# Half sums of eight up weight pairs computed once, early, and stored; the down stage's row loads tied to its fifth step

## Chip, core and metric

The kernel runs on one core of a Trainium2 chip. The metric is device time in microseconds: the median of the runs, 2024.91 us here (3 runs, 2024.34 to 2026.39). The profiled execution is a run of its own, 2030.47 us, of which the profile's span covers 2028.8 us.

The core's engines, as the profile names them: PE (matrix products), PEld (its weight loads), DVE (vector), ACT (scalar, with the activation functions), POOL, and SP, which here only issues transfers. Transfers are issued from SP's, POOL's and ACT's queues. Each engine works its instructions off in a fixed order, and an instruction that waits holds up all that stand behind it on its engine.

## What is computed

One layer of a hybrid decoder on 1024 positions of width 1024, in float32. Cut to what matters:

```
h   = layer_norm(x)
u   = h @ w_in                       # -> conv branch, state-space branch, two gates
y_a = conformer_conv(...)            # 31-tap depthwise convolution, norm, product
y_b = state_space(...)               # 4 groups of 8 heads, in chunks of 128 positions
h   = layer_norm(alpha * h + (sigmoid(ga) * y_a + sigmoid(gb) * y_b) @ w_o)

u   = causal_dwconv3(h @ w_up)       # w_up: 1024 x 5632
gate, val = split(u)                 # 2816 columns each
h   = layer_norm(alpha * h + (silu(gate) * val) @ w_down)
```

## The kernel before

**Products.** A float32 operand is split into two float32r halves (a rounded copy made by ACT, and the remainder, made by a DVE subtraction); a product is the sum of three matrix products (`mm3`, lines 166 to 168). A full matmul works on 128x128 weights and 512 columns.

**Stages.** The positions are worked in two halves of 512. For each half run `ln_in`, `mixers` (all projections, the state-space groups, the convolution), `combine` (gates and the two branches put together, result `mixT`) and an output projection with the second norm. The calls in order are: `ln_in(0)`, `mixers(0)`, `combine(0)`, `ln_in(1)`, then `out_proj` of the first half (rows `r0_0` to `r0_3` in the pool `rows0`), `mixers(1)`, `combine(1)`, and the output projection of the second half inside `ffn_blocks`. Then comes the feed-forward part on all 1024 positions: `up_first`, 22 steps of `up_rest`, and `down`.

**The output stage of the first half.** `out_proj` works the 1024 output columns as two halves q = 0, 1. For each q it takes the four PSUM banks of the pool `pacc` (tag `acc`, four in all), adds up the products of four row blocks t in them with the weights `wo`, and then line 687 adds `r0_t`, the stored first-norm rows, to each bank and writes the sum over `r0_t`. Only this line frees a bank. q = 1 then takes the same banks, and the first products of `mixers(1)` (line 357) after it. The rows `r0_t` come from memory by line 670 on SP's queue.

**SBUF.** Pools opened and closed one after another on the same side lie on the same addresses. `combine` opens its pool at the end of the permanent buffers; its first tiles there are the three `gate` buffers and the two `yb` buffers, 2 KB per partition each. `rows0` opens at the same place: `r0_0`, `r0_1`, `r0_2`, `r0_3` of 4 KB per partition each, then the norm's two rows. The pools are made with `reuse_waits="tile"`: a tile waits for the earlier tiles whose bytes it takes over, and for no others.

**The up stage.** `w_up` and the block of rows are multiplied by a scheme with seven half-size products per step instead of eight. For step j it needs sums of the four quarters of two weight tiles `wup[2j]` and `wup[2j+1]` (512 columns each): `up_weights` loads both tiles (lines 839 and 844), makes four sums of 128x512 on DVE (lines 848 to 851) and splits the results (line 740 on ACT, line 741 on DVE). For the first eight steps (`LEAD`), two of the seven products, those with the unchanged first tile, are done ahead by `up_first`, which stores their sums; in those steps `up_rest` does five products, in the 14 others seven. At a step's end `up_rest` does the convolution and the gate on DVE and ACT and stores the results (lines 919 to 928), from POOL's queue mostly.

**The down stage.** Seven products p of eleven steps k each, in the same manner; `load(p, k)` loads a step's inputs from SP's queue (line 990 the stored up results, line 992 and on the weights). `load_rows(p)` is called at the step k = 4 of p = 0, 1, 2 and 4 and loads 4 quarters of the output's rows each time by line 953 on POOL's queue; with p = 2 also the last norm's two rows. Its transfers wait only for the buffers that they write.

**Order.** A planner lays down each engine's order ahead of the run from a model of the times and from priorities, which follow the program's order, shifted by `tc.high_priority`. A tile takes its buffer when the planner comes to it.

Of the kernel before, what the change touches and what calls it, by code (L numbers as in the profile page):

```python
# [8 lines left out]
F32 = mybir.dt.float32  # L9
# [7 lines left out]
P = 128  # L17
# [39 lines left out]
def kernel(  # L57
# [17 lines left out]
    def pool(name, bufs=1, **kw):  # L75
        return tc.tile_pool(name=name, bufs=bufs, reuse_waits="tile", **kw)
# [60 lines left out]
    h_scr = [dram.tile([HALF, D], F32, name=f"h_scr{i}") for i in range(2)]  # L137
    h1_scr = dram.tile([T, D], F32, name="h1_scr")
    first_scr = [dram.tile([2, P, HALF], F32, name=f"first_scr{j}") for j in range(LEAD)]
    NK = NF // 2  # L140
    b11_scr = [dram.tile([P, HALF], F32, name=f"b11_scr{k}") for k in range(NK)]
    b2_scr, t32_scr, t41_scr = (
# [601 lines left out]
    def ffn_blocks(tp, qp, mixT):  # L744
# [67 lines left out]
            "t4": lambda i: b2[0][:, i, 4:8, :],  # L812
        }

    def up_first(upp, fp, bl, j):

        if j < LEAD - 1:
            t = weights(wup[2 * j], f"ue{j}")
            w = [t[:, i, :] for i in range(2)]
        else:  # L820
            with tc.high_priority(offset=4000):
                st = wst.tile([P, D], F32, tag="st", name=f"st_ue{j}")
                SY.dma_start(st, wup[2 * j])
                w = [upp.tile([P, D], F32R, tag="o", bufs=3, name=f"ue{i}_{j}") for i in range(2)]
                A.copy(w[0], st)
                V.tensor_tensor(out=w[1], in0=st, in1=w[0].bitcast(F32), op=ALU.subtract)
        ps = bank(1)
        for q, block in enumerate(("b11", "b21")):
            product(ps, lambda i: w[i][:, q * HALF : (q + 1) * HALF], bl[block], q == 0)
            f = fp.tile([P, HALF], F32, tag="first", bufs=2, name=f"first{q}_{j}")  # L830
            A.copy(f, ps)
            A.dma_start(first_scr[j][1 - q], f)

    def up_weights(upp, j):


        with tc.high_priority(offset=2000):
            r1 = wst.tile([P, D], F32, tag="st", name=f"ra{j}")
            SY.dma_start(r1, wup[2 * j])
            if j:  # L840
                r2 = upp.tile([P, D], F32, tag="raw", bufs=3, name=f"rb{j}")
            else:
                r2 = wst.tile([P, D], F32, tag="st", name=f"rb{j}")
            SY.dma_start(r2, wup[2 * j + 1])
            a11, a12, a21, a22 = r1[:, :HALF], r1[:, HALF:], r2[:, :HALF], r2[:, HALF:]
            ue = None if j < LEAD else split_pair(wsp, r1, f"ue{j}")
            s3 = upp.tile([P, HALF], F32, tag="s3", name=f"s3_{j}")
            V.tensor_tensor(out=s3, in0=a11, in1=a21, op=ALU.add)
            V.tensor_tensor(out=a21, in0=a21, in1=a22, op=ALU.add)
            V.tensor_tensor(out=a11, in0=a21, in1=a11, op=ALU.add)  # L850
            V.tensor_tensor(out=a12, in0=a12, in1=a11, op=ALU.add)
            w24 = split_pair(wsp, r1, f"s24_{j}")
            w10 = split_pair(wsp, r2, f"s10_{j}")
            w3 = split_pair(upp, s3, f"s3_{j}", HALF, 2)
        return ue, w24, w10, w3
# [74 lines left out]
    def down(upp, dp):  # L930
# [16 lines left out]
        E, L = slice(0, HALF), slice(HALF, D)  # L947
        gb = []

        def load_rows(p):  # L950
            t0, cs = {0: (0, E), 1: (0, L), 2: (4, L), 4: (4, E)}[p]
            for t in range(t0, t0 + 4):
                G.dma_start(rs[t][:, cs], h1_scr[t * P : (t + 1) * P, cs])
            if p == 2:
# [136 lines left out]
        for p, (banks, first, then) in enumerate(products):  # L1091
            end = NK - LAST if p == 6 else NK
            for k in range(end):
# [1 line left out]
                for t in range(4):  # L1095
                    block(banks[t], w, t, first, k)
                if k == 4 and p in (0, 1, 2, 4):
                    load_rows(p)
            ws = {k: load(p, k) for k in range(end, NK)}
            for t in range(4):  # L1100
                for k in ws:
# [12 lines left out]
    hT = ln_in(0)  # L1114
    yT = mixers(0, hT)
    mixT = combine(0, hT, yT)
    hT = ln_in(1)
    with pool("rows0") as pl:
        rs = [pl.tile([P, D], F32, name=f"r0_{t}") for t in range(4)]
# [124 lines left out]
```

## Time and profile before

| | us |
|---|---|
| median of 3 runs | 2024.91 |
| profiled execution | 2030.47 |
| its span | 2028.8 |
| first half up to the output stage | 0 to 636 |
| output stage of the first half, with `ln_in(1)` | 636 to 686 |
| `mixers(1)`, `combine(1)`, second output stage | 686 to 1388 |
| the up steps | 1388 to 1806 |
| the down stage | 1806 to 2028 |

The stages are read from the first and last matmuls of their tiles in the timeline; they overlap a little. Neighbouring full matmuls start 0.227 us apart where PE runs on without a wait (16 of them from 654.83 to 658.23 us, so 15 steps in 3.40 us), though the profile shows each as 0.39 us long, since they overlap. Work on PE is therefore best counted in matmuls, and PE's idle time is what the profile shows between them.

### The profile page before, as it was taken

Reading aid. Unit: us, or ns where it says so; the run is one execution under the profiler, and the core shown is the slowest. Engines: PE = TensorE matmul, PEld = TensorE weight load, DVE = VectorE, ACT = ScalarE, POOL = GpSimd, SP = SyncE. Lnnn points to the kernel's source line nnn. Section 1 sums busy time; section 2 is a strip of 40 time slices with the busy share of each in tenths; the row PEclk is TensorE's granted clock in tenths of the full one; section 3 lists DMA queues with packets and bytes.
Section 4 is the critical chain, followed back from the end, with each engine's and each line's share of the span. In section 5 each row is a group of like instructions: output and inputs, shape, how many; then the busy total and the mean of one; then the engine's idle time right before and its main releaser. Section 6 shows DMA issues by size and latency. Waiting matters only on the chain.

```text
span 2028.8 us, 24542 instructions
## 1 busy us (share of the span) xinstructions
PE 1975.8 (97%) x9164; PEld 1622.4 (80%) x9164; DVE 1695.8 (84%) x2261; ACT 1017.4 (50%) x1480; POOL 175.5 (9%) x140
## 2 busy tenths in 40 slices
PE   7999999999999999999999999999999999999998
PEld 6888888888788888888888888887777777777886
DVE  7599999989766869999998976596897777788768
ACT  4465654556453356665454645364554534443432
POOL 2010101001400000110100130010000000030000
PEclk9999999999999999999999999999999999999999
DMA  6222233333546522222323354565342222367563
GB/s 219 94 64 93 79 103 104 99 104 101 175 131 220 194 94 73 91 81 77 126 89 104 109 167 139 186 234 202 135 172 83 99 107 102 101 252 252 176 225 109
DMA packets 96903, 272.20 MB, mean 134 GB/s; under 512 B 11088, under 2 KB 11088, under 8 KB 96784
## 3 DMA queue, kind: packets, MB, share of 16 engines
q1 hardware_dynamic: 88864, 246.78, 36.8%
q0 software_dynamic: 5616, 19.66, 2.5%
q10 hardware_dynamic: 2304, 4.20, 0.6%
q8 instruction: 72, 1.18, 0.2%
q14 instruction: 47, 0.39, 0.1%
HBM read 221.05 MB, written 49.55 MB: 133 GB/s over the span
## 4 chain that ended last, share of the span: by engine, by line
PE 72%; DVE 19%; DMA 4%; issue 3%; ACT 2%; SPq 0%; DVEq 0%; ACTq 0%
PE acc L166 19%; PE acc L167 19%; PE acc L168 19%; DVE c L420 6%; PE sm L168 3%; PE sm L166 3%; PE sm L167 3%; PE sm L534 2%; PE acc L357 1%; DVE xbc L375 1%; DVE fo L898 1%; DMA dr<-b_scr 1%; PE sm L515 1%; PE sm L192 1%; PE sm L523 1%
## 5 line engine op out<-in xcount | busy, mean ns | idle before, releaser
L420 DVE SCALAR_TENSOR_TENSOR c<-v,pc,c 128x512 f32<-128x512 f32 x480 | 374.9, 804 | 6.3 <-ACT c L409 4.9
L478 POOL TENSOR_TENSOR au<-seg_mv,head_of 128x1024 fp32r<-128x1024 f32 x32 | 76.4, 2388 | 959.1 <-PE sm L487 728.8
L166 PE MATMUL acc<-hT,w_c 128*128 128x512 f32 x352 | 141.0, 401 | 0.0
L167 PE MATMUL acc<-hT,w_c 128*128 128x512 f32 x352 | 140.6, 399 | 0.0
L168 PE MATMUL acc<-hT,w_c 128*128 128x512 f32 x352 | 138.4, 393 | 0.0
L898 DVE SCALAR_TENSOR_TENSOR fo<-u,pc,fo 128x1024 f32<-128x1024 f32 x88 | 111.4, 1279 | 7.5 <-ACT fo L894 7.4
L375 DVE SCALAR_TENSOR_TENSOR xbc<-u,pc,xbc 128x512 f32<-128x512 f32 x144 | 109.9, 775 | 0.7 <-ACT xbc L373 0.5
L166 PE MATMUL acc<-h1s,w_s 128*128 128x512 f32 x264 | 103.6, 396 | 6.3 <-ACT s L880 3.7
L167 PE MATMUL acc<-h1s,w_s 128*128 128x512 f32 x264 | 102.9, 390 | 0.0
L168 PE MATMUL acc<-h1s,w_s 128*128 128x512 f32 x264 | 102.8, 391 | 0.0
L167 PE MATMUL acc<-w_z,hT 128*128 128x512 f32 x256 | 100.8, 394 | 0.0
L166 PE MATMUL acc<-w_z,hT 128*128 128x512 f32 x256 | 100.8, 401 | 0.0
L168 PE MATMUL acc<-w_z,hT 128*128 128x512 f32 x256 | 100.7, 396 | 0.0
L1032 ACT CAST w_dn<-dr 128x1024 fp32r<-128x1024 f32 (+1 forms) x73 | 60.9, 842 | 75.8 <-DVE dr L962 37.8
L154 ACT CAST w_c<-st_c 128x1024 fp32r<-128x1024 f32 x50 | 52.5, 1051 | 88.9 <-PE acc L168 68.2
L1033 DVE TENSOR_TENSOR w_dn<-dr,w_dn 128x1024 fp32r<-128x1024 f32 (+1 forms) x73 | 69.8, 963 | 15.3 <-ACT w_dn L1032 15.1
L167 PEld LDWEIGHTS acc<-hT,w_c 128*128 128x128 f32 x352 | 66.1, 188 | 16.9 <-issue 3.9
L168 PEld LDWEIGHTS acc<-hT,w_c 128*128 128x128 f32 x352 | 66.1, 188 | 16.2 <-issue 2.6
L166 PEld LDWEIGHTS acc<-hT,w_c 128*128 128x128 f32 x352 | 66.1, 188 | 15.9 <-issue 2.6
L166 PE MATMUL acc<-h1b,w_ue 128*128 128x512 f32 x168 | 67.3, 400 | 11.1 <-ACT w_ue L740 8.4
L155 DVE TENSOR_TENSOR w_c<-st_c,w_c 128x1024 fp32r<-128x1024 f32 x47 | 60.5, 1288 | 20.2 <-ACT w_c L154 20.2
L740 ACT CAST w_s<-rb 128x1024 fp32r<-128x1024 f32 x22 | 23.0, 1048 | 98.4 <-PE sm L168 63.8
(353 smaller groups left out, 5755.4 us busy)
## 6 DMA issues: line engine op xcount, KB each, us to landing
st_c<-wcol SPq DMA_DIRECT2D x50, 512.0 KB, 3.5
st_z<-wz SPq DMA_DIRECT2D x32, 512.0 KB, 3.5
st_wo<-wo SPq DMA_DIRECT2D x24, 512.0 KB, 4.0
ra<-wup SPq DMA_DIRECT2D x22, 512.0 KB, 3.6
rb<-wup SPq DMA_DIRECT2D x22, 512.0 KB, 3.4
t_scr<-fo POOLq DMA_DIRECT2D x22, 512.0 KB, 3.8
dr<-t_scr SPq DMA_DIRECT2D x44, 256.0 KB, 3.5
dr<-wdown SPq DMA_DIRECT2D x38, 256.0 KB, 3.9
```

The costliest lines, as they stand in the source:

```text
L154: A.copy(w[:, 0, :], st)
L155: (eng or V).tensor_tensor(out=w[:, 1, :], in0=st, in1=w[:, 0, :].bitcast(F32), op=ALU.subtract)
L166: TE.matmul(ps, wa(0), xa(0), start=start, stop=False, skip_group_check=more)
L167: TE.matmul(ps, wa(0), xa(1), start=False, stop=False, skip_group_check=more)
L168: TE.matmul(ps, wa(1), xa(0), start=False, stop=stop, skip_group_check=more)
L375: V.scalar_tensor_tensor(out=o, in0=u[:, k : k + HALF], scalar=pc[:, wc + k : wc + k + 1], in1=o, op0=ALU.mult, op1=ALU.add,)
L420: V.scalar_tensor_tensor(out=accs[i], in0=v[:, k : k + HALF], scalar=pc[:, wc + k : wc + k + 1], in1=accs[i], op0=ALU.mult, op1=ALU.add,)
L478: G.tensor_tensor(out=au, in0=seg_mv[:, c, :].unsqueeze(1).to_broadcast([P, 8, P]), in1=head_of[:, g, :].unsqueeze(2).to_broadcast([P, 8, P]),
L534: TE.matmul(py[:, hs], m[:, h, :], xs[:, hs], start=True, stop=True)
L898: V.scalar_tensor_tensor(out=o, in0=u[:, k : k + T], scalar=pc[:, wc + k : wc + k + 1], in1=o, op0=ALU.mult, op1=ALU.add,)
L1032: A.copy(w[:, 0, cs], src)
L1033: V.tensor_tensor(out=w[:, 1, cs], in0=src, in1=w[:, 0, cs].bitcast(F32), op=ALU.subtract)
```

## The change

Before `ln_in(1)`, a new function `lead_sums` goes through the first eight pairs: it loads both weight tiles from POOL's queue into one buffer of 10 KB per partition (pool `sums`, one buffer), makes the four half sums on DVE, and stores all five halves in memory (1.25 MB per pair), again from POOL's queue. `up_weights` then loads the finished sums for these steps, in three transfers, instead of the two weight tiles and the four sums; for the other steps the code is the same, except that `r2` and `s3` are taken earlier, and that step 0 takes `r2` from the pool `up` like the others. In `down`, `load_rows` first copies four columns of the step's weight tile `w` into the rows it is about to load, on POOL; the loads then overwrite them, so that they wait for this copy, and the copy waits for `w`.

```diff
+    sums_scr = [dram.tile([P, 2 * D + HALF], F32, name=f"sums_scr{j}") for j in range(LEAD)]
...
+    def lead_sums(pl):
+
+        for j in range(LEAD):
+            r = pl.tile([P, 2 * D + HALF], F32, tag="sums", name=f"sums{j}")
+            for i in range(2):
+                G.dma_start(r[:, i * D : (i + 1) * D], wup[2 * j + i])
+            sums_of_pair(*(r[:, i * HALF : (i + 1) * HALF] for i in range(5)))
+            G.dma_start(sums_scr[j], r)
+
+    def sums_of_pair(a11, a12, a21, a22, s3):
+        V.tensor_tensor(out=s3, in0=a11, in1=a21, op=ALU.add)
+        V.tensor_tensor(out=a21, in0=a21, in1=a22, op=ALU.add)
+        V.tensor_tensor(out=a11, in0=a21, in1=a11, op=ALU.add)
+        V.tensor_tensor(out=a12, in0=a12, in1=a11, op=ALU.add)
+
...
         with tc.high_priority(offset=2000):
             r1 = wst.tile([P, D], F32, tag="st", name=f"ra{j}")
-            SY.dma_start(r1, wup[2 * j])
-            if j:
-                r2 = upp.tile([P, D], F32, tag="raw", bufs=3, name=f"rb{j}")
+            r2 = upp.tile([P, D], F32, tag="raw", bufs=3, name=f"rb{j}")
+            s3 = upp.tile([P, HALF], F32, tag="s3", name=f"s3_{j}")
+            if j < LEAD:
+                ue = None
+                SY.dma_start(r1, sums_scr[j][:, :D])
+                SY.dma_start(s3, sums_scr[j][:, 2 * D :])
+                SY.dma_start(r2, sums_scr[j][:, D : 2 * D])
             else:
-                r2 = wst.tile([P, D], F32, tag="st", name=f"rb{j}")
-            SY.dma_start(r2, wup[2 * j + 1])
-            a11, a12, a21, a22 = r1[:, :HALF], r1[:, HALF:], r2[:, :HALF], r2[:, HALF:]
-            ue = None if j < LEAD else split_pair(wsp, r1, f"ue{j}")
-            s3 = upp.tile([P, HALF], F32, tag="s3", name=f"s3_{j}")
-            V.tensor_tensor(out=s3, in0=a11, in1=a21, op=ALU.add)
-            V.tensor_tensor(out=a21, in0=a21, in1=a22, op=ALU.add)
-            V.tensor_tensor(out=a11, in0=a21, in1=a11, op=ALU.add)
-            V.tensor_tensor(out=a12, in0=a12, in1=a11, op=ALU.add)
+                SY.dma_start(r1, wup[2 * j])
+                SY.dma_start(r2, wup[2 * j + 1])
+                ue = split_pair(wsp, r1, f"ue{j}")
+                sums_of_pair(r1[:, :HALF], r1[:, HALF:], r2[:, :HALF], r2[:, HALF:], s3)
...
-        def load_rows(p):
+        def load_rows(p, w):
             t0, cs = {0: (0, E), 1: (0, L), 2: (4, L), 4: (4, E)}[p]
+            G.tensor_copy(
+                rows.rearrange("p (t n) -> p t n", n=D)[:, t0 : t0 + 4, cs.start : cs.start + 1],
+                w[:, 0, :4].bitcast(F32).unsqueeze(2),
+            )
             for t in range(t0, t0 + 4):
                 G.dma_start(rs[t][:, cs], h1_scr[t * P : (t + 1) * P, cs])
...
                 if k == 4 and p in (0, 1, 2, 4):
-                    load_rows(p)
+                    load_rows(p, w)
...
     mixT = combine(0, hT, yT)
+    with pool("sums") as pl:
+        lead_sums(pl)
     hT = ln_in(1)
```

## The prediction

> **What bounds the kernel now.** I read the page first: busy time, then the chain, then windows around the three places that the change touches.
>
> ```profile
> span 2028.8 us, 24542 instructions
> ...
> PE 1975.8 (97%) x9164; PEld 1622.4 (80%) x9164; DVE 1695.8 (84%) x2261; ACT 1017.4 (50%) x1480; POOL 175.5 (9%) x140
> ...
> PE 72%; DVE 19%; DMA 4%; issue 3%; ACT 2%; SPq 0%; DVEq 0%; ACTq 0%
> ```
>
> PE is busy for 97% of the span, and the change takes no matmul away. So all that can be gained is PE's idle time, 2028.8 - 1975.8 = 53 us, and what is done to other engines counts only where PE waits for it. The windows say where the idle time lies at the three places.
>
> ```profile
> core 0: us, PE busy (x) PEld busy (x) DVE busy (x) ACT busy (x) POOL busy (x), PEclk, DMA share, GB/s
> 636.50:661.80 25.30, 24.09 (x114) 19.78 (x112) 18.91 (x28) 8.62 (x13) 0.00 (x0) 1.00 0.87 332
> 661.80:686.30 24.50, 23.67 (x112) 19.79 (x113) 19.89 (x30) 6.81 (x10) 0.00 (x0) 1.00 0.49 176
> ...
> 1432.00:1512.00 80.00, 72.65 (x308) 56.52 (x307) 68.14 (x78) 40.18 (x50) 3.95 (x7) 1.00 0.44 155
> ...
> 1819.00:1832.00 13.00, 9.62 (x36) 7.55 (x35) 6.08 (x9) 5.70 (x10) 0.97 (x2) 0.83 0.94 346
> ```
>
> The first two rows are the output stage of the first half (q = 0, then q = 1): PE is idle for 1.2 and 0.8 us. The third is most of the eight short up steps: 7.4 us idle in 80, with DVE at 85%. The last is the start of the down stage: 3.4 us idle, the granted clock at 0.83, the DMA engines at 94%.
>
> **Part 1: the sums moved early, and what they stand in front of.** The buffer `sums` takes 10 KB per partition at the place where `combine` had three `gate` and two `yb` buffers of 2 KB: exactly those bytes. So the first load waits for the last reader of `gate`. After it, `rows0` opens at the same place: `r0_0` and `r0_1` lie wholly, `r0_2` in half on the bytes of `sums`. There is one buffer, so the eight pairs go one after another: load, four adds, store, and only when the store has landed the next load. The rows `r0_0` to `r0_2` can be loaded only after the eighth store. Who waits for them?
>
> ```profile
> 637.62 0.69 DVE L661 TENSOR_TENSOR mb<-mb,gl 128x512 f32<-128x512 f32 x1
> ...
> 661.82 1.86 DVE L687 SCALAR_TENSOR_TENSOR r<-r,acc 128x512 f32<-128x512 f32 x3
> ...
> 660.69 1.09 PE L192 MATMUL sm<-ident,x 128*128 128x128 f32 x8 [1.19 <-DVE x L230]
> 662.63 0.47 PE L166 MATMUL acc<-w_wo,mixT 128*128 128x512 f32 x1 [0.85 <-DVE r L687]
> ```
>
> The first row is the last use of `gate`: the chain of sums can start at 637.62 + 0.69 = 638.3 us. The last row is the point that decides: the first product of q = 1 waits for line 687, which frees the bank by adding `r0_t`. All four banks of `acc` are held by q = 0 until then, and the products of q = 1 and of `mixers(1)` take their banks from the same four. So from 662.6 us on PE stands until the eighth store has landed, a row has been loaded and line 687 has run, apart from 24 of the 32 transposes of `ln_in(1)`, which use other banks (8 took 1.09 us, so 3.3 us). `r0_3` lies beyond the buffer and may come early; one bank serves one row block of q = 1, and three weight buffers hold 18 of its products, 4.1 us; I count that as a bound only.
>
> Now the length of the chain. These are rows of transfers of the same kind:
>
> ```profile
> L928 POOL DMA_DIRECT2D t_scr<-fo x6: 531/531/533, 1552.0 to 1752.5; - x6
> ...
> DMA to landing us min/median/max: 2.9/3.5/4.3
> ...
> b_scr<-fo POOLq DMA_DIRECT2D x11, 256.0 KB, 2.3
> ...
> ra<-wup SPq DMA_DIRECT2D x22, 512.0 KB, 3.6
> ...
> r<-h_scr SPq DMA_DIRECT2D x4, 512.0 KB, 10.9
> ...
> L848 DVE TENSOR_TENSOR s<-ra,rb 128x512 f32<-128x512 f32 x22 | 15.1, 684 | 1.6 <-DMA rb<-wup 1.6
> ```
>
> - Loads: two of 512 KB, the second issued 0.53 us after the first. `ra`, the same tile from the same array, lands after 3.6 us: 0.5 + 3.6 = 4.1 us; with the slowest `t_scr` transfer (4.3) 4.8 us. I take 4.4.
> - Adds: 4 x 0.684 = 2.7 us, and a little for two hand-overs: 3.0 us. If DVE is busy with other work that stands ahead, up to 4.
> - Store of 1.25 MB: no such transfer is in the trace. Two `t_scr` stores of 512 KB, issued 0.53 us apart, are down after at most 0.5 + 4.3 = 4.8 us, and that for 1 MB: lower end 4.8 us. By the step from 256 KB (2.3) to 512 KB (3.5), 1.2 us for each 256 KB, it is 2.3 + 4 x 1.2 = 7.1 us: upper end. I take 5.4, near the pair, which is the nearest in size.
>
> One pair: 4.4 + 3.0 + 5.4 = 12.8 us; ends 4.1 + 2.7 + 4.8 = 11.6 and 4.8 + 4 + 7.1 = 15.9. The first pair meets the inputs of `ln_in(1)`, where 512 KB took 10.9 us to land (the row of `r`); I give it 18 us (14 to 20). The chain ends at 638.3 + 18 + 7 x 12.8 = 745.9 us. A row lands about 3.6 us later, line 687 takes 0.7: PE goes on at 750.2 instead of 662.6, 87.6 us late. Of that 3.3 us of transposes go off.
>
> The Trainium skill, "DMA: Bandwidth & Descriptors", section "Anatomy of one DMA — SWDGE (gpsimd) path", gives 2.0 us and the bytes by 436 GB/s for one transfer. By it, as an estimate, the load pair is 4.4 us and the store 5.0, so that the chain would end some 3 us earlier. Its rule for kernel authors, to overlap a transfer with work, speaks against a chain with one buffer.
>
> PE is also slow after a stop:
>
> ```profile
> 1391.46 0.79 PE L166 MATMUL acc<-h1b,w_ue 128*128 128x512 f32 x1 [2.73 <-ACT first L831]
> 1392.05 0.63 PE L167 MATMUL acc<-h1b,w_ue 128*128 128x512 f32 x1
> ...
> 1396.32 0.63 PE L168 MATMUL acc<-h1b,w_ue 128*128 128x512 f32 x1
> ```
>
> After 2.73 us of idle time, 12 steps took 1396.74 - 1391.46 = 5.3 us (the next matmul starts at 1396.74) where they take 12 x 0.227 = 2.7: 2.6 us lost. I add that once. **Part 1 costs 87.6 - 3.3 + 2.6 = +87 us**; with pairs at 11.6 and the first at 14 it is 87 - 4 - 8 = +75, less 4 if `r0_3` serves early: +71; with 15.9 and 20, +87 + 2 + 22 = +111.
>
> ```profile
> 740.12 3.34 POOL L478 TENSOR_TENSOR au<-seg_mv,head_of 128x1024 fp32r<-128x1024 f32 x1 [185.25 <-DVE seg_mv L328]
> ```
>
> What else is moved: the 32 adds (22 us of DVE) fall into a time in which DVE would wait for PE, so nothing. On POOL, `lead_sums` stands ahead of the `au` products of `mixers(1)`, the first at 740.12 us; they wait for `mixers(1)` itself and move with it, so nothing. SP's loads that the planner puts behind the `r0` loads wait with them; three weight buffers are filled ahead, which covers the first 3 x 24 matmuls of the next products, so nothing, or 4 us if it puts the `wo` loads behind. The stage after, `mixers(1)`, cannot make the time good: its work on PE is unchanged.
>
> **Part 2: the up steps.** The four adds per step go (4 x 0.684 = 2.7 us of DVE), for eight steps.
>
> ```profile
> 1466.97 0.54 POOL L919 DMA_DIRECT2D b_scr<-fo  x1 [12.38 <-DVE fo L909]
> ...
> 1527.79 0.55 POOL L919 DMA_DIRECT2D b_scr<-fo  x1 [11.26 <-DVE fo L909]
> ...
> PE acc L166 <- ACT s L880: 3.0, 4, 0.9
> PE acc L166 <- ACT u L883: 2.4, 2, 1.7
> PE sm L166 <- ACT w_s L740: 2.0, 3, 1.3
> ```
>
> Line 919 stores once per two steps: four steps take 60.8 us, 15.2 each, where 60 matmuls need 60 x 0.227 = 13.6. That is the 7.4 us of idle time, with the slow restarts. PE waits for ACT each time: 3.0 us for a bank's copy at line 880, which also stays in the long steps' order and may remain; the other 4.4 us are ACT held up behind DVE or behind the sums (line 740 casts `s3` right after line 848). I take -6 us for the eight steps: 4.4 us of these, and part of line 880. Bounds: 0, if the planner's new order keeps the waits, and 8 x 1.6 = -13. The loads grow from two to three per step and from 1 to 1.25 MB; the DMA share there is 0.44, so nothing.
>
> **Part 3: the row loads.**
>
> ```profile
> 1781.99 4.63 POOL L993 COPY c<-dr 128x512 f32<-128x512 f32 x4 [12.34 <-PE acc L168]
> ...
> 1805.38 3.78 POOL L953 DMA_DIRECT2D rows<-h_scr  x7 [1.70 <-PE sm L168]
> ...
> rows<-h_scr POOLq DMA_DIRECT2D x16, 256.0 KB, 8.2
> ...
> 1827.85 0.62 ACT L1032 CAST w_dn<-dr 128x512 fp32r<-128x512 f32 x1 [7.30 <-DMA dr<-b_scr]
> ...
> PE acc L166 <- ACT w_dn L1032: 3.4, 1, 3.4
> ```
>
> All 16 row loads (4 MB) are issued from 1805 us on, as the down stage begins; a stored up result comes 7.3 us late for its cast, and PE stands for 3.4 us and restarts slowly (2.6 us as above): 6.0 us. With the copies only four of the 16 can go at the start, 3 MB fewer ahead of the late load, about 9 us at the 346 GB/s of the last window row. So most of the 6.0 goes: I take -4, bounds 0 (the weights `c` and the remaining rows still crowd it) and -6. The four POOL copies of 128x4 cost less than the 128x512 copies of line 993 (four in 4.63 us, 1.2 each), off PE's path. Behind a waiting copy on POOL stand the row loads themselves, the last up pair's two stores and the last norm's rows; the stores are needed from p = 2 on, a product of 11 x 12 matmuls (30 us) after, so nothing; a row load that came late would hold up `then(t)` seven steps (19 us) later.
>
> **Sum.** 2030.5 + 87 - 6 - 4 = 2107.5 for the profiled execution, which lay 5.6 us above the median: **2102 us** for the median.
>
> **The rivals.**
>
> 1. *The wait is longer.* Pairs of 16 to 20 us, because stores of 10 KB rows are slow or DVE's laid-down order holds the adds behind waiting work. Against it: nothing else runs on the DMA engines once PE stands. With 18 us: +87 + 7 x 5.2 = +123, less 10: 2138 us.
> 2. *The wait is partly covered.* PE is given products of `mixers(1)` or of q = 1 during the chain. For it: the planner knows the wait. Against it: these need banks of `acc`, and only `r0_3` can free one. If half the wait went: 2025 + 43 - 10 = 2058 us.
> 3. *Faster: the rows do not wait for the sums*, because `rows0` does not come to lie on the buffer. Then the chain runs beside PE, and parts 2 and 3 are left: 2025 - 10 = 2015 us. It is decided by addresses alone: as soon as one of `r0_0` to `r0_2` shares bytes with `sums`, it falls. For it speaks only that the trace shows no addresses; the sizes (3 + 2 buffers of 2 KB, opened at the same place) speak against it.
> 4. *The change does less than it says*: the wait as forecast, but the new order gives no gain in parts 2 and 3: 2112 us, inside the forecast's range.
>
> **How the numbers follow.** Chances: the forecast (with 4) 0.74, longer wait 0.10, partly covered 0.07, faster 0.09. The forecast's own range: 2024.9 + 71 - 19 = 2077 to 2024.9 + 111 = 2136. With some us for a new order elsewhere, the range for 8 in 10 is 2071 to 2139: it leaves out rivals 2 and 3 nearly whole and half of rival 1. Runs of this kernel differ by 0.1%, so about 0.2% (4 us) can be told from no change. Faster by more: 0.09; within: 0.01; slower: 0.90.
>
> **What would show it.** Right: PE idle from about 666 to 750 us with line 687 and behind it the load of `r` as releaser; eight stores to `sums_scr` 12 to 13 us apart; the granted clock down in those slices; 14 instead of 22 of each add in the up stage, and its idle time (1432 to 1512 before) at 2 us or less; row loads in four groups, no wait of 3 us at the start of the down stage. Wrong: products of `mixers(1)` between 662 and 750 us, stores closer than 11 us, or the `r` loads ahead of the last of them.

## The result and the profile after

The changed kernel takes **2131.36 us** (median of 4 runs, 2130.93 to 2132.63), the kernel before 2025.65 us (4 runs); the ratio is **1.052** with a 95% interval of 1.0504 to 1.0535. The forecast was 2102 us, with a range of 2071 to 2139 us. Line numbers are those of the kernel that a row is from; in the changed kernel line 687 has become 688, line 166 has become 167 and line 919 has become 934.

The page of the changed kernel, busy time and chain of waits:

```profile
span 2130.9 us, 24619 instructions
...
PE 1979.5 (93%) x9164; PEld 1626.5 (76%) x9164; DVE 1701.1 (80%) x2261; ACT 1019.2 (48%) x1480; POOL 190.2 (9%) x168
...
PE 62%; DVE 24%; DMA 7%; issue 4%; ACT 2%; POOL 0%; SPq 0%; DVEq 0%; ACTq 0%; POOLq 0%
```

The span has grown by 102.1 us and PE's busy time by 3.7 only, so nearly all of it is PE standing still. The chain says through whom: PE has fallen from 72% to 62% of a longer chain, DMA has risen from 4% to 7%, DVE from 19% to 24%. The timeline of PE, then POOL, SP and DVE around the output stage of the first half (start, duration, idle time before and what ended it):

```profile
663.12 3.75 PE L193 MATMUL sm<-ident,x 128*128 128x128 f32 x16 [3.44 <-DVE x L231]
672.83 3.65 PE L193 MATMUL sm<-ident,x 128*128 128x128 f32 x16 [5.96 <-DVE x L231]
773.76 0.77 PE L167 MATMUL acc<-w_wo,mixT 128*128 128x512 f32 x1 [97.29 <-DVE r L688]
...
640.08 1.24 POOL L821 DMA_DIRECT2D sums<-wup  x2 [84.14 <-ACT mixT L183]
666.93 0.54 POOL L823 DMA_DIRECT2D sums_scr<-sums  x1 [25.62 <-DVE sums L829]
672.34 1.06 POOL L821 DMA_DIRECT2D sums<-wup  x2 [4.87 <-DMA sums_scr<-sums]
683.51 0.54 POOL L823 DMA_DIRECT2D sums_scr<-sums  x1 [10.11 <-DVE sums L829]
688.54 1.05 POOL L821 DMA_DIRECT2D sums<-wup  x2 [4.49 <-DMA sums_scr<-sums]
697.16 0.54 POOL L823 DMA_DIRECT2D sums_scr<-sums  x1 [7.57 <-DVE sums L829]
702.18 1.05 POOL L821 DMA_DIRECT2D sums<-wup  x2 [4.49 <-DMA sums_scr<-sums]
...
764.73 0.54 POOL L823 DMA_DIRECT2D sums_scr<-sums  x1 [7.36 <-DVE sums L829]
...
769.59 1.75 SPq L671 DMA_DIRECT2D r<-h_scr  x4
...
649.53 1.29 DVE L208 BATCH_NORM_STATS2 st_in<-x 128x6 f32<-128x512 f32 x2 [8.41 <-DMA x<-x]
...
656.90 0.68 DVE L826 TENSOR_TENSOR sums<-sums 128x512 f32<-128x512 f32 x1
...
680.34 0.69 DVE L826 TENSOR_TENSOR sums<-sums 128x512 f32<-128x512 f32 x1 [2.52 <-DMA sums<-wup]
...
694.00 0.69 DVE L826 TENSOR_TENSOR sums<-sums 128x512 f32<-128x512 f32 x1 [10.78 <-DMA sums<-wup]
...
772.93 0.69 DVE L688 SCALAR_TENSOR_TENSOR r<-r,acc 128x512 f32<-128x512 f32 x1 [8.49 <-DMA r<-h_scr]
```

Read from the bottom: line 688 waits for a row, the four rows are issued at 769.59 us, which is 4.9 us after the eighth store was issued at 764.73, and PE goes on 4.2 us later. Before the change the first product of q = 1 (the third row) went off at 662.63 us; now it goes off at 773.76, **111.1 us later**. The POOL rows are the chain itself: each load waits for the store before it. A whole pair of the steady part is 688.54 to 702.18: load to the first add 5.5 us, adds and hand-over 3.2, store 5.0. The DVE row's 10.78 us of idle time is a store and a load in one, not a load of 11 us. How long the chain's loads took to land, all 16 of line 821 (then all of the chain's stores, with their size and median):

```profile
DMA to landing us min/median/max: 3.9/4.7/8.6
...
sums_scr<-sums POOLq DMA_DIRECT2D x8, 1280.0 KB, 4.7
```

The windows of the changed kernel (stretch, its length, busy us per engine, granted clock, DMA share, GB/s): the stop, the short up steps from the first b_scr store to that of j = 6, and the start of the down stage.

```profile
661.80:780.00 118.20, 13.53 (x48) 11.09 (x49) 39.55 (x57) 5.18 (x10) 11.66 (x22) 0.54 0.55 204
1543.90:1636.40 92.50, 87.85 (x371) 69.89 (x370) 74.27 (x80) 48.89 (x60) 4.85 (x9) 0.98 0.46 154
1919.00:1945.00 26.00, 26.00 (x116) 21.51 (x116) 23.71 (x35) 13.17 (x24) 6.82 (x14) 1.00 0.90 304
```

```profile
1433.70:1527.80 94.10, 86.75 (x369) 68.18 (x368) 80.82 (x93) 48.84 (x62) 5.02 (x10) 1.00 0.42 149
```

The last row is the same up stretch of the kernel before: PE was idle there for 7.4 us, and now for 4.7. At the start of the down stage PE no longer stands at all. So both small gains came, and the stop outweighs them. Where the time lies, by the distance of the same event in the two traces:

| event | before | after | distance |
|---|---|---|---|
| first product of the output stage after line 688 | 662.63 | 773.76 | +111.1 |
| b_scr store of j = 0 | 1433.73 | 1543.87 | +110.1 |
| b_scr store of j = 6 | 1527.79 | 1636.43 | +108.6 |
| b_scr store of j = 20 | 1803.13 | 1911.70 | +108.6 |
| end (span) | 2028.8 | 2130.9 | +102.1 |

The last product of the second half's output stage, just ahead of the up stage, stands at +112.6. So Part 1 cost about 112 us, Part 2 gave back 4.0, and Part 3 gave back 6.5; the three add up to the span's 102.1 by the way they are read. The 4.0 is a rough figure: in the kernel with the early sums alone (below), whose up steps are those of the kernel before, the distance shrinks over the same stretch too, from 111.6 to 109.0 us.

### The profile page after: what moved, and what is told of

It reads as the page before. It is cut to its first block, busy times and chain, and to the rows that moved or that the text cites. A ratio compares the mean times of both kernels' runs of the same rounds, so it can differ in the third digit from the quotient of the medians.

```text
span 2130.9 us, 24619 instructions
## 1 busy us (share of the span) xinstructions
PE 1979.5 (93%) x9164; PEld 1626.5 (76%) x9164; DVE 1701.1 (80%) x2261; ACT 1019.2 (48%) x1480; POOL 190.2 (9%) x168
## 4 chain that ended last, share of the span: by engine, by line
PE 62%; DVE 24%; DMA 7%; issue 4%; ACT 2%; POOL 0%; SPq 0%; DVEq 0%; ACTq 0%; POOLq 0%
PE acc L167 16%; PE acc L168 16%; PE acc L169 16%; DVE c L421 8%; PE sm L167 3%; PE sm L168 3%; PE sm L169 3%; DMA sums_scr<-sums 2%; DMA sums<-wup 2%; DVE xbc L376 2%; PE acc L358 1%; PE sm L535 1%; DVE fo L913 1%; DMA st_wo<-wo 1%; PE sm L516 1%
## 5 line engine op out<-in xcount | busy, mean ns | idle before, releaser
L167 PE MATMUL acc<-w_wo,mixT 128*128 128x512 f32 x128 | 49.2, 402 | 98.5 <-DVE r L688 97.3
L167 PEld LDWEIGHTS acc<-w_wo,mixT 128*128 128x128 f32 x128 | 24.6, 193 | 104.8 <-issue 97.7
L155 ACT CAST w_wo<-st_wo 128x1024 fp32r<-128x1024 f32 x24 | 25.4, 1057 | 155.2 <-PE acc L169 145.9
L168 PEld LDWEIGHTS acc<-hT,w_c 128*128 128x128 f32 x352 | 66.1, 188 | 16.9 <-issue 3.8
L1052 DVE TENSOR_TENSOR w_dn<-dr,w_dn 128x1024 fp32r<-128x1024 f32 (+1 forms) x73 | 69.8, 963 | 11.2 <-ACT w_dn L1051 10.9
L169 PEld LDWEIGHTS acc<-hT,w_c 128*128 128x128 f32 x352 | 66.1, 188 | 16.1 <-issue 2.6
```

The lines of the kernel that those rows point to most:

```text
L155: A.copy(w[:, 0, :], st)
L167: TE.matmul(ps, wa(0), xa(0), start=start, stop=False, skip_group_check=more)
L168: TE.matmul(ps, wa(0), xa(1), start=False, stop=False, skip_group_check=more)
L169: TE.matmul(ps, wa(1), xa(0), start=False, stop=stop, skip_group_check=more)
L1052: V.tensor_tensor(out=w[:, 1, cs], in0=src, in1=w[:, 0, cs].bitcast(F32), op=ALU.subtract)
```

## The experiments

Eleven kernels ran, one of them twice. Times are medians, and ratios are against the kernel before on the same chip, with 95% intervals; a time without a ratio is one run.

| kernel | time | before there | ratio |
|---|---|---|---|
| early sums alone (not used) | 2139.18 | 2028.87 | |
| sums for four pairs | 2079.05 | 2028.87 | |
| buffer above the rows | 2086.63 | 2028.87 | 1.0284 (1.0269 to 1.0299) |
| row copies alone | 2023.60 | 2028.87 | 0.9971 (0.9960 to 0.9982) |
| row copies, one burst | 2023.54 | 2028.54 | 0.9978 (0.9968 to 0.9987) |
| three loads, no sums | 2024.27 | 2028.54 | 0.9984 (0.9976 to 0.9993) |
| above the rows, adds on POOL | 2058.18 | 2028.54 | 1.0141 (1.0127 to 1.0156) |
| above the rows, two buffers, late priority | 2066.03 | 2028.54 | |
| two buffers on the rows | 2099.68 | 2028.02 | |
| early, on POOL, in cc's bytes | 2035.88 | 2028.02 | 1.0036 (1.0022 to 1.0050) |
| the same, four pairs | 2027.06 | 2027.77 | 0.9993 (0.9984 to 1.0001) |
| row copies alone, again | 2022.82 | 2027.77 | 0.9977 (0.9967 to 0.9986) |

### Does the cost come from the sums, and from the bytes?

Two kernels ask whether Part 1 is alone to blame, and whether the shared bytes are the reason. The first is the kernel before with nothing but the early sums, whose results nobody reads:

```diff
     mixT = combine(0, hT, yT)
+    with pool("sums") as pl:
+        lead_sums(pl)
     hT = ln_in(1)
```

> The kernel before with only lead_sums put in; what it stores is not read. Theory: the wait alone, 112 us on the way from the output stage to the first products of mixers(1), and nothing given back: 2025.7 + 112 = 2138 us. Rival (the up steps or the row loads add to the loss, and the wait is smaller): below 2125 us.

It took 2139.18 us, 110.3 more than before, and PE goes on after line 688 at 773.83 us, where the changed kernel has 773.76:

```profile
773.83 0.77 PE L167 MATMUL acc<-w_wo,mixT 128*128 128x512 f32 x1 [97.49 <-DVE r L688]
```

So Part 1 makes the stop by itself. The second moves the buffer above the rows:

```diff
-    with pool("sums") as pl:
-        lead_sums(pl)
-    hT = ln_in(1)
     with pool("rows0") as pl:
+        with pool("sums") as sp:
+            lead_sums(sp)
+        hT = ln_in(1)
         rs = [pl.tile([P, D], F32, name=f"r0_{t}") for t in range(4)]
```

> The same work in the same program order, but the pool rows0 is opened before the pool sums, so that the buffer of the sums lies above the rows and r0_0 to r0_3 share no byte with it. Theory (shared bytes make the rows wait for the eighth store): the chain of eight pairs stays (12 to 16 us a pair from about 640 to 755 us), but PE goes on with q = 1 at about 663 us, and what is left is the gain of the other two parts: 2025.7 - 4 - 6.5 = 2015 us, ratio 0.995. Rival (the chain's transfers, its adds on DVE or its place in POOL's queue hold up the output stage, wherever the buffer lies): PE still stands for tens of us after 662 us, and the time stays above 2090 us.

The ratio is 1.0284: the 2015 us of the theory were missed by 72, and the rival's 2090 were not reached either. The wait for `r` is gone: the rows are issued at 646.40 us instead of 769.59, and the first product of q = 1 goes off at 664.57 us, 1.9 later than before the change. But another wait has come. SP's queue in the timeline of this kernel, PE's wait (total, times, longest), then ACT and DVE in the timeline:

```profile
646.40 6.55 SPq L671 DMA_DIRECT2D r<-h_scr  x4
...
PE acc L167 <- ACT w_z L155: 57.2, 1, 57.2
...
783.37 0.31 ACT L283 ACTIVATE sp<-sp 128x128 f32<-128x128 f32 x1 [64.55 <-DVE sp L282]
...
725.70 0.69 DVE L826 TENSOR_TENSOR sums<-sums 128x512 f32<-128x512 f32 x1 [10.09 <-DMA sums<-wup]
...
780.18 0.69 DVE L826 TENSOR_TENSOR sums<-sums 128x512 f32<-128x512 f32 x1 [10.83 <-DMA sums<-wup]
...
783.05 0.28 DVE L282 COPY sp<-sm 128x128 f32<-128x128 f32 x1
```

DVE is idle for ten us ahead of each of the last five pairs and does nothing else meanwhile, since the planner laid their adds in one row ahead of lines 281, 282 and 376, which `mixers(1)` needs. Line 282 takes its turn at 783.05 us, after the last add; ACT has waited for it for 64.6 us, and PE for ACT. The Trainium skill, "TensorE: Matmul & The Clock Gate", section "Architectural detail: the array is 16× 32×32, not 1× 128×128", says that ScalarE and VectorE take their instructions strictly in order. These rows agree. So the shared bytes carry the stop in the changed kernel, and the adds on DVE are a second cost behind it, here 57.2 us of PE's waiting, which the longer stop hid.

### Does the length of the chain set the stop?

Sums for four pairs instead of eight, the other four as before:

```diff
-        for j in range(LEAD):
+        for j in range(4):
             r = pl.tile([P, 2 * D + HALF], F32, tag="sums", name=f"sums{j}")
...
-            if j < LEAD:
+            if j < 4:
                 ue = None
```

> The changed kernel with four pairs in lead_sums instead of eight; steps 4 to 7 load their weight tiles and make the sums as before. Theory (the wait is the sum of the pairs, one after another): four pairs of 13.5 us less, 2131.4 - 54 = 2077 us, and about 2 us of the up steps' gain lost: 2079 us. Rival (a fixed hold-up, such as the planner's order of the output stage): about 2130 us.

PE goes on at 718.16 us, 55.6 us earlier than in the changed kernel; four pairs of 13.5 us are 54. The time is that of the theory.

```profile
718.16 0.77 PE L167 MATMUL acc<-w_wo,mixT 128*128 128x512 f32 x1 [43.73 <-DVE r L688]
```

Next, a second buffer at the same place:

```diff
-    with pool("sums") as pl:
+    with pool("sums", bufs=2) as pl:
         lead_sums(pl)
```

> The whole change with a second buffer beside the first, still on the bytes of the rows, adds on DVE. My theory: the stop on PE is as long as the chain, and the chain is load, adds, store one after the other only because there is one buffer; with two, the next load runs beside the store, 8 to 9 us a pair from the second pair on instead of 13.55, and PE goes on some 30 to 40 us earlier: 2090 to 2102 us. Rival: the transfers are bound by the DMA engines rather than by their order (2.25 MB a pair), or POOL's queue keeps them serial: above 2120 us.

It took 2099.68 us, and PE goes on 30.8 us earlier than with one buffer; both lie where the theory had them. PE and POOL in the timeline of this kernel, first and last store:

```profile
742.99 0.77 PE L167 MATMUL acc<-w_wo,mixT 128*128 128x512 f32 x1 [64.17 <-DVE r L688]
...
668.73 0.54 POOL L823 DMA_DIRECT2D sums_scr<-sums  x1 [26.70 <-DVE sums L829]
...
730.15 0.54 POOL L823 DMA_DIRECT2D sums_scr<-sums  x1 [9.97 <-DVE sums L829]
```

From the first to the eighth store it is 61.4 us, 8.8 for each pair where one buffer gives 13.4 to 16.6. The first store comes no earlier than with one buffer (666.93 us). So the time of a pair comes from load, adds and store standing one after another, and the first pair is another matter: its adds wait for their turn on DVE, which works at `ln_in(1)` then (see the part on what was mis-sized).

### Are Parts 2 and 3 worth what the distances say?

The row copies alone, in the kernel before:

```diff
-        def load_rows(p):
+        def load_rows(p, w):
             t0, cs = {0: (0, E), 1: (0, L), 2: (4, L), 4: (4, E)}[p]
+            G.tensor_copy(
+                rows.rearrange("p (t n) -> p t n", n=D)[:, t0 : t0 + 4, cs.start : cs.start + 1],
+                w[:, 0, :4].bitcast(F32).unsqueeze(2),
+            )
...
```

> The kernel before with only the copies in load_rows. Theory (fewer transfers at the start of the down stage): no wait of PE for a cast at the start of the down stage, 6 to 6.5 us less, 2019 us, ratio 0.997. Rival (the 6.5 us between the last up store and the end of the down stage came from the new order that follows from the up part): the wait of 3.4 us stays and the time is within 2 us of before.

The ratio is 0.9971, and 0.9977 when it ran again (below): 4.7 to 5.9 us less. PE has no wait left between 1800 and 1860 us, so the theory's sign is there. Why it gains is asked by the next kernel, which issues all 16 loads at the first of the four places:

```diff
-                if k == 4 and p in (0, 1, 2, 4):
-                    load_rows(p, w)
+                if k == 4 and p == 0:
+                    for q in (0, 1, 2, 4):
+                        load_rows(q, w)
```

> The row copies alone, but all 16 row loads are issued together, after the fifth step of the first product (each group still behind its copy). My theory: what the row loads alone gained (ratio 0.997) came from taking 3 MB away from in front of the late stored up result at the start of the down stage; then one burst, though it begins some 20 us later than before the change, meets other loads of the first and second product, and at least half of the gain goes: ratio 0.998 to 1.001, with waits on dr or w_dn somewhere between 1820 and 1860 us. Rival: the gain comes from the later start (the burst no longer falls on the last stored up results) or from the planner's new order, and spreading is worth nothing: ratio 0.997 again.

The ratio is 0.9978, and this interval and that of the copies alone overlap for the most part. The theory's waits between 1820 and 1860 us are not there: PE waits for nothing from 1800 to 1860 us. So the rival is right, and spreading is worth nothing that can be told here. POOL's timeline and a window of this kernel:

```profile
1809.32 10.27 POOL L952 COPY rows<-w_dn 128x4 f32<-128x4 f32 x4 [7.24 <-ACT w_dn L1036]
1819.53 4.34 POOL L957 DMA_DIRECT2D rows<-h_scr  x8
...
1820.00:1840.00 20.00, 20.00 (x90) 16.57 (x89) 16.00 (x26) 9.72 (x18) 9.87 (x19) 1.00 1.00 349
```

and the same window of the kernel before:

```profile
1820.00:1840.00 20.00, 16.62 (x61) 13.17 (x60) 12.07 (x19) 7.32 (x15) 2.70 (x5) 0.83 0.89 307
```

With one burst the DMA engines are full from 1820 to 1840 us, and PE does not stop once. The burst begins at 1819.53 instead of 1805.38 us, behind the six loads of stored up results that SP issues from 1808.69 us on, instead of ahead of them. Part of that is the copies' own length: four of them take 10.27 us here, where one takes 0.19 to 0.59 us in the kernel with the copies alone. That the later start is what counts fits these rows, but it is not shown by itself: the planner's new order, which the rival named beside it, came with the same edit. And in the kernel with the copies alone the first four loads start at 1810.74 us already, only 5.4 us later than before the change, with twelve fewer behind them.

For Part 2 there is the kernel before with three loads and no adds in the eight steps. It leaves out the sums, so it serves for the time alone:

```diff
...
+            if j < LEAD:
+                ue = None
+                SY.dma_start(r1, wup[2 * j])
+                SY.dma_start(s3, wup[2 * j][:, :HALF])
+                SY.dma_start(r2, wup[2 * j + 1])
...
```

> The kernel before with the up part alone: in the first eight up steps three loads (the half for s3 is read from the weights themselves) and no adds; the sums of the first eight pairs are left out, and neither the early sums nor the row copies are there. My theory, by the traces of the whole change (time between the last product of the second output stage and the up store of j = 20, 4.0 us shorter): about 4 us less, ratio 0.998, with 2.7 us less idle time on PE in the eight steps. The recorded prediction: 6 us less, 0.997. Rival: the planner's new order gives it back, 1.000.

The ratio is 0.9984: 3.2 us less (1.4 to 4.9). PE's waits from 1432 to 1528 us, where the kernel before had 7.4 us of them (3.0 for line 880, 2.4 for line 883, 2.0 for line 740), now lines 895, 898 and 741 of this kernel:

```profile
PE acc L167 <- ACT u L898: 3.7, 4, 1.5
PE sm L167 <- ACT w_s L741: 1.8, 2, 1.5
PE acc L167 <- ACT s L895: 0.7, 1, 0.7
```

The wait for the copy of `s` shrinks from 3.0 to 0.7 us. Those for `u` and `w_s` stay: of the 3.7 us for `u`, 1.5 lie at 1433.87 us, ahead of the first `b_scr` store (1434.97 us), so that the stretch itself, from that store to the one of j = 6, holds 2.2 where it held 2.4 before. Together that is 4.7 us, as in the changed kernel. So the adds had held up the copy of `s`; what holds the other two was not tried.

### Can the sums be had for nothing?

If the stop is a matter of place and engine, a version should exist in which only the gains are left. The first try keeps the buffers above the rows, takes two, gives the sums a lower priority for the planner, and gives the adds to POOL:

```diff
+        with pool("sums", bufs=2) as sp:
+            with tc.high_priority(offset=-1500):
+                lead_sums(sp)
...
-            sums_of_pair(*(r[:, i * HALF : (i + 1) * HALF] for i in range(5)))
+            sums_of_pair(*(r[:, i * HALF : (i + 1) * HALF] for i in range(5)), G)
```

> The whole change with the sums taken off both waits: two buffers, above the rows so that no byte is shared with r0, and the 32 adds on POOL instead of DVE. My theory: what was left at 1.028 with the buffer above the rows was DVE held by adds ahead of the products of the next mixers; with the adds on POOL (1.61 us each by the POOL adds of the same size in the combine stage, 6.5 us a pair; about 11 us a pair with the transfers, so the chain ends near 740 us, when POOL's first au product is due) nothing is held: the up steps' 4 and the row loads' 6 us are left, ratio 0.995 (2015 us). Rival: POOL's chain runs past 740 us and holds the au products, or POOL's adds slow DVE: 1.00 to 1.02.

The ratio is 1.0141, and the theory missed. The rival's range holds it, but the longest wait has a cause that neither named. ACT's timeline in this kernel:

```profile
727.20 0.19 ACT L373 COPY u<-u_halo 128x3 f32<-128x3 f32 x1
753.03 0.69 ACT L374 ACTIVATE xbc<-acc,pc 128x512 f32<-128x512 f32 x1 [25.65 <-DMA sums_scr<-sums]
```

It is the first mechanism once more, with another tile. In the built program the two buffers reach to byte 168,288 of a partition, and one of the first `xbc` tiles of `mixers(1)` begins at byte 168,000. ACT waits for the last store, 25.7 us. (One buffer at this place ends at 158,048, which is why the kernel above did not meet it.) It is not the whole loss: the first product of `mixers(1)`, ahead of this wait, already stands at 699.53 instead of 686.33 us. The same two buffers with the adds left on DVE:

```diff
+        with pool("sums", bufs=2) as sp:
+            with tc.high_priority(offset=-1500):
+                lead_sums(sp)
```

> As the version with the buffer above the rows, but with two buffers and with the sums at a lower priority for the planner, adds still on DVE. My theory (DVE held by the adds in its laid-down order until their loads come): the chain is shorter (store beside load, 8 to 9 us a pair) and the adds of pairs 3 to 7 stand between products of the next mixers, so the hold shrinks from 58 us to 15 to 35 us: 2035 to 2060 us. Rival: the hold is not DVE's order, then it stays at 2087 us.

2066.03 us: less than 2087, but above the expected 2060, and for a reason that was not expected. PE's longest wait in this stretch is for `xbc` again (24.2 us), not for DVE's order alone.

The second try goes earlier. A pad puts two buffers on the bytes of the `cc` tiles of `combine`, free from about 576 us on, and POOL, which is idle from 555 to 740 us before the change, does the adds:

```diff
     mixT = combine(0, hT, yT)
...
+    with pool("pad") as pad, pool("sums", bufs=2) as sp:
+        pad.tile([P, 6656], F32, name="pad")
+        lead_sums(sp)
...
```

> The whole change with the sums at another place and on another engine: two buffers on the bytes of combine's cc tiles (free from about 570 us; a pad of 26 KB below them keeps them off the four rows), the adds on POOL, which does nothing from 555 to 740 us in the kernel before. My theory: both holds seen so far come from what stands behind the sums, first in memory (r0 in the changed kernel, xbc with the sums above the rows on POOL), then in DVE's order. With about 13 us a pair the chain runs from about 575 to 680 us, before the next mixers write their first xbc tiles at about 690 and before POOL's first au product: nothing waits, and Part 2 (3 to 4 us) and Part 3 (6 us) are left: 2015 to 2019 us, ratio 0.995 to 0.997. Rival: the 18 MB of sums' transfers hold up the loads of the output stage (the x rows and their norm, as in the version on POOL above the rows, where PE waited 18.7 us for x): 1.00 to 1.01.

The ratio is 1.0036: of the changed kernel's 106 us all but some 7 are gone, but it is still slower than before. No tile waits for the sums, and the last store is issued at 682.50 us. POOL's first `au` product runs at 754.84 instead of 740.12 us, 14.7 us later, and the two gains do not make such a loss good. PE's waits from 640 to 755 us in this kernel, then POOL and DVE in its timeline:

```profile
PE sm L193 <- DVE mv_in L222: 5.8, 1, 5.8
PE sm L193 <- DVE x L231: 4.4, 2, 4.2
...
657.11 2.22 POOL L826 TENSOR_TENSOR sums<-sums 128x512 f32<-128x512 f32 x1 [6.71 <-DMA sums<-wup]
...
656.91 3.51 DVE L228 SCALAR_TENSOR_TENSOR x<-x,mv_in,in_g 128x1024 f32<-128x1024 f32 x2 [0.41 <-DMA in_g<-prow]
660.34 2.28 DVE L156 TENSOR_TENSOR w_wo<-st_wo,w_wo 128x1024 fp32r<-128x1024 f32 x1
```

These are inputs of `ln_in(1)`. (The 18.7 us for `x` that the expectation names are that kernel's total over its whole run; in this stretch it waits 5.4 us for `x` and 5.4 for `mv_in`.) I put the waits down to the sums' transfers beside the `x` loads, and tested it with four pairs (in `up_weights` too), whose last store is issued at 623.45 us:

```diff
-        for j in range(LEAD):
+        for j in range(4):
```

> As the early sums on POOL in combine's bytes, but for four pairs only; the up steps 4 to 7 load and add as before the change. In the version with eight, four pairs were stored by 629 us, and POOL's first au product came 14.7 us later than in the kernel before, which I put down to the sums' transfers of pairs 5 to 8 beside the x loads (640 to 690 us). My theory: with no transfer of sums after 640 us that delay is gone, and half of Part 2 (2 us) and Part 3 (6 us) are left: 2018 to 2022 us where before is at 2028, ratio 0.996. Rival: the delay has another cause (POOL's work, or the loads that SP issues), then at least half of it stays: 1.000 or more.

The ratio is 0.9993, between the theory and the rival and nearer to the rival. POOL's `au` product is on the rival's side too, with 10.3 of the 14.7 us left (750.40 us), but PE is not: its first product of `mixers(1)`, at 686.33 us before the change, stands at 692.03 with four pairs and at 698.16 with eight, so 5.7 of 11.8 us stay. What stays is there although the loads are not late: DVE waits 5.89 us for the first `x`, where it waited 5.95 us before. PE, then DVE, in the timeline of this kernel:

```profile
666.45 1.94 PE L193 MATMUL sm<-ident,x 128*128 128x128 f32 x8 [5.10 <-DVE x L231]
...
646.70 1.29 DVE L208 BATCH_NORM_STATS2 st_in<-x 128x6 f32<-128x512 f32 x2 [5.89 <-DMA x<-x]
...
658.98 1.23 DVE L231 SCALAR_TENSOR_TENSOR x<-x,rs_in,in_b 128x1024 f32<-128x1024 f32 x1
665.03 1.28 DVE L231 SCALAR_TENSOR_TENSOR x<-x,rs_in,in_b 128x1024 f32<-128x1024 f32 x1
666.22 0.68 DVE L688 SCALAR_TENSOR_TENSOR r<-r,acc 128x512 f32<-128x512 f32 x1
```

DVE is busy without a gap from 655 to 670 us in both kernels. Before the change it had freed the first bank (line 687) at 661.82 us, behind two rows of `x`; here it turns to line 688 at 666.22, behind three. So DVE's order of work is another one, and PE waits for it. That the planner lays it out anew because of the sums is likely; it was not tried by itself.

What the other four pairs add is not order: from the first `x` to line 688 DVE runs the same instructions in the same order in both kernels, from 646.70 to 666.22 us with four pairs and from 649.04 to 673.05 with eight. The eight-pair kernel starts 2.3 us later, waits 0.4 us for `in_g`, and takes some 4 us more for four instructions that run while POOL adds: 2.16 to 2.31 us each instead of 1.22 to 1.28. Its first product of q = 1 goes off 6.8 us later (674.87 against 668.05). By these rows some 2.7 of them are late loads, as I had put it, and some 4 are POOL's adds slowing DVE, which was the rival of the kernel with the adds on POOL above the rows and which I had not looked for.

The row copies alone, the same edit as above, ran beside it:

> The row copies alone once more, beside the four early pairs on the same chip: 0.997 as measured before. If the four early pairs are worth their 2 us, they come out 0.001 below this; within the intervals otherwise.

0.9977, 3 to 4 us better than the four early pairs. So the best kernel of the study is the one with **the row copies and no early sums**: 0.9971 and 0.9977 of the time before.

## Why the prediction was right, and what was mis-sized

The direction, the place and the mechanism were as forecast, and 2131 us lies in the range of 2071 to 2139, but near its upper end: 29 us above the forecast, 24 of them in one chain. Part 1 by itself came out at 112 us, just outside the +71 to +111 that I gave it. The total stayed inside because the upper end had counted Parts 2 and 3 at nothing, and they gave back 10.5 us: here the range held by its width.

| term of Part 1 | forecast | measured | difference |
|---|---|---|---|
| chain starts | 638.3 | 640.08 | +1.8 |
| first pair | 18 (14 to 20) | 672.34 - 640.08 = 32.3 | +14.3 |
| second pair | 12.8 | 688.54 - 672.34 = 16.2 | +3.4 |
| six more pairs | 6 x 12.8 = 76.8 | 769.59 - 688.54 = 81.1 | +4.3 |
| row and line 688 | 4.3 | 773.76 - 769.59 = 4.2 | -0.1 |
| PE goes on | 750.2 | 773.76 | +23.6 |

- **Part 1, the first pair: outside its own bounds, and for another reason than the one I gave.** I took the load at the 10.9 us of a row among the inputs of `ln_in(1)` and added the usual adds and store. But no load of line 821 took longer than 8.6 us to land (shown with the result), and the pair's second one was issued at 640.78: both tiles were there by 649.4 us. The first add ran at 656.90, 7.5 us later, with DVE busy all the time since 649.53 at work that stood ahead of it, and from there to the store it took another 10.0 us, because the four adds took turns with `ln_in(1)`. That is 17.5 us from the landing to the store where I had 3.0, with "up to 4" as the bound. The term that failed is the adds' turn on DVE, not the load. The store itself took 5.4 us. The second pair is another case: its adds ran in one row, and its 3.4 us too many are the load, 8.0 us from the first issue (672.34) to the first add (680.34).
- **Part 1, the steady pair:** 5.46 + 3.16 + 5.02 = 13.6 us against 4.4 + 3.0 + 5.4. The 1.25 MB store lands after 4.7 us in the median, just below my lower end of 4.8, which was the price of two stores of 512 KB. The load pair was priced too low; it came out above the 4.8 that I gave as its slow end. The Trainium skill, "DMA: Bandwidth & Descriptors", section "Anatomy of one DMA — SWDGE (gpsimd) path", has 5.0 us for the store as an estimate; the trace agrees within 0.3. For the load pair, taken as one transfer of 1 MB, it has 4.4, and the trace, with 5.5 to the first add, does not agree.
- **Part 1, the credit for transposes (-3.3) and the slow restart (+2.6):** the restart is as forecast. After the stop 13 matmuls take 779.44 - 773.76 = 5.7 us instead of 13 x 0.227 = 3.0. With the credit and a restart of 2.7, the 111.1 at the restart would be 110.5 at the first product of `mixers(1)`; there it is 112.0, so half of the credit did not show.
- **Part 1, the rivals:** no product of q = 1 or `mixers(1)` came into the stop, so rival 2 falls; the rows waited, so rival 3 falls. Rival 1 has a true half: DVE's laid-down order held the first pair's adds. The pairs of 16 to 20 us that it priced did not come, except the second, and that one because of its load.
- **Part 2:** -6 forecast, -4.0 in the trace, -3.2 (1.4 to 4.9) alone. The step that failed is "part of line 880" beside the whole of the other 4.4 us: line 880's wait nearly went (3.0 to 0.7 us), and the waits for `u` and `w_s` stayed (2.4 to 2.2 and 2.0 to 1.8); the stretch kept 4.7 us of idle time where I had named 2 or less.
- **Part 3:** -4 forecast (0 to -6), -6.5 in the trace, -4.7 to -5.9 alone. The size was fair. The reason, "3 MB fewer ahead of the late load", is not the one that carries the gain: the single burst issues all 16 loads together, later, and gains as much. Whether its later start or the planner's new order does it stays open.

With the measured terms the sum is 2030.5 + 112 - 4 - 6.5 = 2132.0, and the profiled execution took 2132.6; that they agree says nothing more, since the terms were read from these two traces. Of the 29 us between forecast and median, 25 are these terms (2132.6 - 2107.5); the other 4 come from the profiled execution before, which lay 5.6 us above its median where this one lies 1.2 above.

## What to carry to other kernels

Work that is moved into a gap takes a place in memory as well as in the queues: ask which tile comes next on its bytes and what stands behind it in each engine's order, and count the whole serial chain until the last transfer lands, since the next owner waits for that and not for the engine's idle time. A chain of transfers is easiest to mis-price at its first link, where it meets the stage around it: ask there not only when its loads land but when the engine gets to its adds, since what is laid ahead of them runs first. Work that is given to another engine can still slow the first one. And when a burst of loads delays something, try to start it later before spreading it.

## What was not expected of the hardware

- One store of 1.25 MB landed in 4.7 us in the median, where the 22 `t_scr` stores of 512 KB in the same kernel took 3.8: 2.5 times the size for a quarter more time. Seven of the eight large stores had the DMA engines nearly to themselves, the small ones did not.
- With the DMA engines at a share of 1.00 (349 GB/s) from 1820 to 1840 us, PE stayed 100% busy; at a share of 0.89 in the kernel before it stood for 3.4 us.
- The same add of 128x512 on POOL varies by two thirds within one run. In the version above the rows with the adds on POOL, the eight adds from 730 us on, while DVE ran nothing, took 1.25 to 1.29 us each; those of 2.1 us and more all lie beside DVE instructions of 128x1024 with two tiles as inputs, nearly all of which then took 1.7 to 2.5 us instead of 1.2 to 1.3. So the two engines slow each other here. The rows (ns: minimum, median, maximum) of one add's line in that kernel, with DVE's own beside it:

```profile
L826 DVE TENSOR_TENSOR s<-ra,rb x14: 682/686/693, 1526.7 to 1776.0; 128x512 f32<-128x512 f32 x14
L826 POOL TENSOR_TENSOR sums<-sums x8: 1255/1297/2173, 651.4 to 742.6; 128x512 f32<-128x512 f32 x8
```
